# Gates A and B and the MLP's up projection as seven products of halves, with their splits spread over two units

## The chip, the cores and the metric

The kernel runs on one core of a Trainium2 chip. The metric is the device time of one execution in microseconds (us). The kernel before takes 857.63 us, the median of three runs (856.81 to 858.55).

## The reference

One encoder layer is applied to two groups of 256 tokens, so to 512 tokens of 1024 features, all in float32. Cut to what matters here:

```
proj = rms_norm(x) @ w_in          # q, k, v of three attention branches, and three gates ga, gb, gm of 1024 each
merged = sigmoid(ga) * (oa @ w_branch_a) + sigmoid(gb) * (ob @ w_branch_b) + sigmoid(gm) * (om @ w_branch_m)
x = x + merged @ w_out
x = x + square(relu(rms_norm(x) @ w_up)) @ w_down      # w_up 1024 x 4096, w_down 4096 x 1024
return rms_norm(x)
```

## The kernel before

**Layout and splits.** Activations stand with features on the 128 partitions and the 512 tokens along the free dimension. A float32 product is made of three matmuls in fp32r: every operand is split into a high part, which ScalarE (ACT) writes as a rounded copy, and a low part, which VectorE (DVE) writes as the operand less the high part. `mm3` issues high times high, high times low and low times high into one PSUM bank. `fm` runs `mm3` over the k tiles with a 128x128 piece of a weight as the stationary operand and all 512 tokens as the moving one. So a tile of 128 features costs 8 x 3 = 24 matmuls of 512 columns.

**Weights.** A weight comes in chunks of 128x1024 (512 KB) through SP's DMA queue into one of two `raw` buffers; ACT writes `hi`, then DVE `lo`, into ten `w` buffers (five chunks). During attention GpSimd (POOL) writes the `lo`s.

**Order of the work.** The program is one list of units, and `run` calls them in turn. Each unit may name sources; `run` fetches those of later units `ahead` sources early (three in the stages below). The engines are kept in the order of the calls (`InOrder`), so the order of the list is the order on PE, DVE and ACT. `later` holds evictions of a product until `flush` in the next unit; `lows` holds low parts until `lower()`, which `run` calls ahead of each unit.

**Gates and branches** (from 326 us on). Gate M was projected during attention. For each of eight feature tiles `ff` stand two units `gate` (24 matmuls of 512 columns each, then a sigmoid) and one unit `branches`, which multiplies the three attention outputs `OA`, `OB`, `OM` by their weights, times the gates. The sums go to POOL. `merge` splits the result into `M`; the last tile is split directly ahead of the output projection (`out_proj`), which reads all eight tiles.

**MLP.** The up projection makes 32 feature tiles (`up`, two halves of 12 matmuls each), four for each of eight blocks c of the down projection. The down projection of a block is seven products (Strassen's method on a 2 x 2 cut of tokens and features): `form` makes the activations' sums and differences, `parts` the weights' ones. There the weights' sums are made by DMAs that add onto a tile in SBUF (`accum_op`, on POOL's queue): `load_blocks` loads four blocks, and `T` grows block by block as its earlier products are split. Each product is 12 matmuls of 512 columns. A half of `up` and one `product` alternate; `add_to` adds the products into accumulators in SBUF. The last block c = 7 is multiplied directly (`last_down`), the sums enter the residual (`combine`, `sum_in`), and `finish`, `gained`, `factor` and `scale_out` make the final norm.

Of the kernel before, what the change touches and what calls it, by code (L numbers as in the profile page):

```python
# [16 lines left out]
P = 128  # L17
# [60 lines left out]
def encoder_kernel(ctx: ExitStack, tc: tile.TileContext, a: dict, out: bass.AP):  # L78
# [94 lines left out]
    def lower(keep=0):  # L173
        for fn in lows[:len(lows) - keep]:
            fn()
        del lows[:len(lows) - keep]

    def run():
        need = [(i, s) for i, (_, srcs) in enumerate(units) for s in srcs]
        got, at = [[] for _ in units], 0  # L180
        done = 0
        for i, (fn, srcs) in enumerate(units):
            done += len(srcs)
            for fetch in (True, False):
                while at < min(len(need), done + (0 if fetch else ahead[0])):
                    u, s = need[at]
                    got[u].append(s[0]() if callable(s[0]) else chunk(*s))
# [573 lines left out]

    MG, wb, sg = [], [], {}

    def gate(w, ff, br):
        p = bank()
        fm(w, X, p)
        g = h2("g")
        A.activation(g, p, AF.Sigmoid)
        sg[ff, br] = g

    def branches(w, *more):
        ff = len(MG)
        if more:
            wb[:] = more
        A.activation(GM[ff], GM[ff], AF.Sigmoid)
        sg[ff, 2] = GM[ff]
        c0 = (ff % 4) * 256
        parts = ((w[0][:, :512], w[1][:, :512], OA), (wb[0][0][:, c0:c0 + 256], wb[0][1][:, c0:c0 + 256], OB),
                 (w[0][:, 512:], w[1][:, 512:], OM))
        for br, (wh, wl, O) in enumerate(parts):  # L780
            p = bank()
            fm((wh, wl), O, p)
            V.tensor_tensor(sg[ff, br], p, sg[ff, br], op=ALU.mult)
        eng = V if ff == KD - 1 else G
        eng.tensor_tensor(sg[ff, 0], sg[ff, 0], sg[ff, 1], op=ALU.add)
        eng.tensor_tensor(sg[ff, 0], sg[ff, 0], sg[ff, 2], op=ALU.add)
        MG.append(sg[ff, 0])
# [3 lines left out]
    def merge(*ks):  # L791
        for k in ks:
            x = s4("mg")
            A.activation(x[:, 0], MG[k], AF.Copy)
            (V, G)[k % 2 if k < KD - 1 else 0].tensor_tensor(x[:, 1], MG[k], f(x[:, 0]), op=ALU.subtract)
            M.append(x)

    for ff in range(KD):
        for br in range(2):
            unit(lambda w, ff=ff, br=br: gate(w, ff, br), (a["w_g"][ff, br],))  # L800
        if ff == KD - 1:
            unit(lambda: merge(*range(KD - 1)))
        unit(branches, (a["w_bam"][ff],), *([(a["w_bb"][ff // 4],)] if ff % 4 == 0 else []))


    unit(lambda: merge(KD - 1))


    X1, H = [], []

    def out_proj(w):
        ff = len(H)
        r = h2("xr")
        A.dma_start(r, a["xT"][:, ff])
        p = bank()
        fm(w, M, p)
        V.tensor_tensor(r, p, r, op=ALU.add)
        X1.append(r)
        x = s4("h")
        A.activation(x[:, 0], r, AF.Copy, scale=gains[:, 2, ff:ff + 1])  # L820
        V.scalar_tensor_tensor(x[:, 1], r, gains[:, 2, ff:ff + 1], f(x[:, 0]), op0=ALU.mult,
                               op1=ALU.subtract)
        H.append(x)

    for ff in range(KD):
        unit(out_proj, (a["w_o"][ff],))

# [9 lines left out]

    def mlp_pool():
        stages.close()
        at[0] = stages.enter_context(tc.tile_pool(name="ml", bufs=1))

    def block_tile():
        return at[0].tile([P, 1024], F32, tag="blk", name=nm("blk"), bufs=8)
# [23 lines left out]
    def up(w, ff, half):  # L871

        if half == 0:
# [28 lines left out]
    def load_blocks(c):  # L902
# [3 lines left out]
        t = {n: block_tile() for n in "T2BC"}  # L906
        for n, b in (("T", "11"), ("2", "21"), ("C", "12"), ("B", "22")):
# [4 lines left out]
    def parts(c, n):  # L912

        def go():
            load_blocks(c)
            hi, lo = w_tile(), w_tile()
            src = blocks[c][n[0]]
            A.activation(hi, src, AF.Copy)

            def low():  # L920
                V.tensor_tensor(lo, src, f(hi), op=ALU.subtract)
                if n[1:]:
                    G.dma_start(src, block(c, n[1:]), accum_op=ALU.add)  # L923

            lows.append(low)
# [5 lines left out]
    def form(c, name):  # L931
# [11 lines left out]
        elif name == "Q5":  # L943
            src = forms[c, "S1"] = less(A21, A22)
        elif name == "Q6":
            src = forms[c, "S2"] = less(A11, forms.pop((c, "S1")))
        elif name == "P7":
            src = less(A11, A21)
        else:
            src = less(A12, forms.pop((c, "S2")))  # L950
        x = s4("f")
        xh, xl = (x[:, i].rearrange("p (j t) -> p j t", j=2) for i in range(2))
        A.activation(xh, src, AF.Copy)
        lows.append(lambda: V.tensor_tensor(xl, src, f(xh), op=ALU.subtract))
        forms[c, name] = x

    acc, banks = {}, {}
# [9 lines left out]
    PRODUCTS = dict(P1=("T12", "a", "V", -1), P2=("2", "a", "11", 1), Q5=("T22", "d", "G", 1),  # L967
                    Q6=("T21", "c", "V", 1), P7=("C", "e", "G", -1), Q3=("B", "d", "12", 1), Q4=("T", "e", "21", 1))

    def product(w, c, name):  # L970
        _, bk, to, sign = PRODUCTS[name]
# [47 lines left out]
    def last_down(hh, ts, n0=0, n1=512, part=0):  # L1019
        flush(9)  # L1020
        lower()
# [36 lines left out]
    unit(mlp_pool)  # L1058
    ORDER = ("P1", "P2", "Q5", "Q6", "P7", "Q3", "Q4")


    SUMMED = {1: ("12", "12"), 2: ("11", "11"), 3: ("21", "21"), 4: ("12", "V"), 5: ("21", "V", 1), 6: ("22", "G")}

    def make(c, n):
        unit(lambda: form(c, ORDER[n]))

    for c in range(NC):
        for h in range(8):
            ff, half = 4 * c + h // 2, h % 2
            unit(lambda *w, ff=ff, half=half: up(w[0] if w else None, ff, half), *([(a["w_up"][ff],)] if half == 0 else []))  # L1070
            if c == 0:
# [106 lines left out]
```

## Time and profile before

| | |
|---|---|
| median of three runs | 857.63 us |
| the profiled execution | 859.08 us |
| its span, first to last instruction | 857.3 us |
| mean granted TensorE clock | 0.993 |
| bytes moved by DMA | 106.87 MB |

The page of the profile lists for each engine the busy time, its share of the span and the instructions. PE is TensorE's matmuls, PEld its weight loads, which overlap the matmuls. A group row reads: line, engine, operation, output<-inputs, shapes, count | busy us, mean ns of one | idle time of the engine just before them, and what ended it. A row of the timeline reads: start, length, engine, operation, count, and in brackets the idle time before it with its releaser. Nearly all instructions have line 72, the helper that keeps the order; tiles tell them apart. A matmul's recorded length holds its way through the array, so the pace is read from start to start.

### The profile page before, as it was taken

How to read it: one execution, taken by the hardware profiler on the slowest of the kernel's cores; microseconds unless marked ns; L12 is line 12 of the kernel's file. 1: busy time of each engine (PE TensorE's matmuls, PEld its weight loads, DVE VectorE, ACT ScalarE, POOL GpSimd, SP SyncE). 2: the span in 40 equal slices, each digit the busy share in tenths (PEclk: the TensorE clock that was granted, in tenths of full speed). 3: DMA queues.
4: the chain of work that ended last, by engine and by line, in shares of the span. 5: the costliest groups of instructions: out<-in, count | busy, mean ns of one | idle time of the engine just before them, and what ended most of it. 6: DMA issues, size and time to landing. Idle time of an engine off the chain costs nothing.

```text
span 857.3 us, 10785 instructions
## 1 busy us (share of the span) xinstructions
PE 844.4 (99%) x4080; PEld 703.8 (82%) x4080; DVE 462.8 (54%) x737; ACT 397.1 (46%) x690; POOL 216.0 (25%) x161
## 2 busy tenths in 40 slices
PE   9999999999999999999999999999999999999996
PEld 7788998888888888888888788888888888888885
DVE  6575535465452311423435542465767666767895
ACT  6455545565554333222323227564445353545453
POOL 2314554656556543211123000000000000000001
PEclk9999999999999999999999999999999999999998
DMA  8343122324241228432322445374747465645322
GB/s 284 115 119 109 62 99 86 98 63 115 85 119 64 75 74 286 132 99 86 110 99 74 147 147 161 110 204 107 205 109 208 111 185 121 178 120 172 75 75 98
DMA packets 47468, 106.87 MB, mean 125 GB/s; under 512 B 19358, under 2 KB 19604, under 8 KB 47416
## 3 DMA queue, kind: packets, MB, share of 16 engines
q1 hardware_dynamic: 39992, 85.69, 30.2%
q0 software_dynamic: 4256, 14.73, 9.7%
q10 hardware_dynamic: 3168, 5.77, 2.0%
q8 instruction: 32, 0.52, 0.3%
q14 instruction: 20, 0.16, 0.1%
HBM read 101.93 MB, written 4.24 MB: 124 GB/s over the span
## 4 chain that ended last, share of the span: by engine, by line
PE 84%; DVE 8%; ACT 5%; issue 2%; DMA 1%; POOL 0%; POOLq 0%; SPq 0%; DVEq 0%; ACTq 0%
PE ps L72 77%; PE sc L72 3%; PE o L72 2%; DVE w L72 2%; PE tp L72 2%; ACT w L72 2%; DVE f L72 1%; ACT sp L72 1%; DVE sp L72 1%; DMA mr<-in_memT 1%; ACT f L72 1%; DVE sq L72 0%; ACT r L72 0%; DVE mg L72 0%; DVE acc L72 0%
## 5 line engine op out<-in xcount | busy, mean ns | idle before, releaser
L72 PE MATMUL ps<-x,w 128*128 128x512 f32 x1080 | 252.5, 391 | 0.0
L72 PEld LDWEIGHTS ps<-x,w 128*128 128x128 f32 x1080 | 201.0, 188 | 41.3
L72 PE MATMUL ps<-h,w 128*128 128x512 f32 x768 | 184.5, 391 | 0.0
L72 PEld LDWEIGHTS ps<-h,w 128*128 128x128 f32 x768 | 143.7, 188 | 29.5
L72 PE MATMUL ps<-w,f 128*128 128x512 f32 (+1 forms) x696 | 164.1, 387 | 1.3 <-DVE acc L72 1.0
L72 DVE TENSOR_TENSOR w<-raw,w 128x1024 fp32r<-128x1024 f32 (+1 forms) x79 | 96.4, 1223 | 115.3 <-ACT w L72 115.2
L72 PEld LDWEIGHTS ps<-w,f 128*128 128x128 f32 x696 | 128.7, 188 | 29.9 <-issue 3.4
L72 ACT ACTIVATE w<-raw 128x1024 fp32r<-128x1024 f32 (+2 forms) x116 | 119.7, 1036 | 21.9 <-DMA raw<-in_w_mem 7.5
L161 POOL TENSOR_TENSOR w<-raw,w 128x1024 fp32r<-128x1024 f32 (+1 forms) x37 | 87.3, 2361 | 120.1 <-ACT w L72 94.9
L72 DVE TENSOR_TENSOR w<-blk,w 128x1024 fp32r<-128x1024 f32 x49 | 59.5, 1224 | 47.7 <-ACT w L72 47.6
L923 POOL DMA_DIRECT2D blk<-in_w_dn x21 | 18.1, 864 | 240.2 <-DVE w L72 240.2
L72 ACT ACTIVATE w<-blk 128x1024 fp32r<-128x1024 f32 x49 | 50.7, 1047 | 15.4 <-DMA blk<-in_w_dn 15.4
L72 DVE TENSOR_TENSOR acc<-acc,ps 128x512 f32<-128x512 f32 x82 | 52.9, 682 | 2.9 <-PE ps L72 2.9
L72 ACT ACTIVATE f<-f 128x512 fp32r<-128x512 f32 x28 | 17.7, 633 | 75.4 <-DVE f L72 75.4
L72 ACT ACTIVATE sp<-sp,st 128x256 f32<-128x256 f32 (+1 forms) x48 | 25.8, 538 | 57.7 <-DVE st L72 57.7
L72 ACT ACTIVATE g<-ps 128x512 f32<-128x512 f32 x16 | 9.6, 598 | 88.4 <-PE ps L72 88.4
L72 DVE TENSOR_TENSOR sum<-o,lo 64x256 f32<-64x256 f32 x24 | 10.0, 417 | 66.5 <-ACT lo L72 66.3
L72 PE MATMUL ps<-mg,w 128*128 128x512 f32 x192 | 44.2, 391 | 1.5 <-ACT mg L72 0.9
L72 PEld LDWEIGHTS ps<-mg,w 128*128 128x128 f32 x192 | 36.0, 188 | 9.6 <-ACT mg L72 1.3
L72 ACT ACTIVATE r<-ps 128x512 f32<-128x512 f32 x32 | 18.9, 591 | 50.7 <-PE ps L72 50.7
L72 PE MATMUL ps<-w,x 128*128 128x384 f32 (+1 forms) x192 | 39.9, 363 | 0.0
L469 POOL TENSOR_TENSOR sp<-sp,st 128x512 f32<-128x512 f32 (+1 forms) x32 | 36.7, 1147 | 6.5 <-DVE st L72 3.6
(146 smaller groups left out, 959.2 us busy)
## 6 DMA issues: line engine op xcount, KB each, us to landing
raw<-in_w_up SPq DMA_DIRECT2D x32, 512.0 KB, 4.7
blk<-in_w_dn SPq DMA_DIRECT2D x28, 512.0 KB, 6.7
blk<-in_w_dn POOLq DMA_DIRECT2D x28, 512.0 KB, 5.7
raw<-in_w_g SPq DMA_DIRECT2D x24, 512.0 KB, 3.3
raw<-in_w_b SPq DMA_DIRECT2D x12, 512.0 KB, 3.3
raw<-in_w_bam SPq DMA_DIRECT2D x8, 512.0 KB, 3.3
raw<-in_w_o SPq DMA_DIRECT2D x8, 512.0 KB, 3.2
raw<-in_w_mem SPq DMA_DIRECT2D x7, 512.0 KB, 3.3
```

Source lines behind the costliest of these rows:

```text
L72: return self.tc.keep_in_program_order(method(*args, **kw))
L161: sub[0].tensor_tensor(lo[:, c], raw[:, c], f(hi[:, c]), op=ALU.subtract)
L469: G.tensor_tensor(s[:, :, :w], s[:, :, :w], st[:, 6:8].unsqueeze(2).to_broadcast([P, 2, w]), op=ALU.mult)
L923: G.dma_start(src, block(c, n[1:]), accum_op=ALU.add)
```

## The change

Gates A and B, and 28 of the 32 tiles of the up projection, are made as seven products of halves as well. `seven` takes four feature tiles at a time and cuts 1024 input features, 512 output features and 512 tokens into halves. One product is 24 matmuls with 256 tokens as the moving operand, seven products take the place of 96 matmuls of 512 columns. `halves_of` makes the four sums of the activations once for the gates and once for the up projection; `take` adds the products up. The weights' sums are DMAs that add onto a tile, as in the down projection; their rows come as two pieces of 512 columns. Gates run in two groups `q` of four tiles, A and B in turn; the four tiles of block c = 0 of `up` stay as they were.

The branch of M comes first, as eight units of its own (`memory_branch`), then gates of group 0, branches A and B, gates of group 1, branches A and B. The sums of the branches go from POOL to DVE. The first two tiles of `out_proj` are made together, the last two k tiles of both at the end. In the down projection two of the weight blocks come through `raw` in place of tiles of their own.

`lower` is replaced by `tick`, called at the start of a unit: it runs the weights' low parts (`wlows`), then the activations' low parts (`lows`), then the steps put off to ACT (`soon`). So a sum that DVE makes in one unit is copied by ACT in the next and lowered by DVE in the one after.

```diff
+    def tick():
+
+        for todo in (wlows, lows, soon):
+            now = todo[:]
+            todo.clear()
+            for fn in now:
+                fn()
...
+        def go(n, w):
+            tick()
+            new = n in ("P1", "Q5", "Q6", "P7")
+            if new:
+                banks[BANK[n]] = bank()
+            b = banks[BANK[n]]
+            for j in range(2):
+                for k in range(4):
+                    c = slice(j * 512 + k * P, j * 512 + (k + 1) * P)
+                    xh, xl = form_of(X, forms, n, k)
+                    mm3(b[:, j * S:(j + 1) * S], w[0][:, c], w[1][:, c], xh, xl, new and j == k == 0, k == 3, j > 0 or not new)
+            flush(9)
+            later.append(lambda: take(n, b))
...
+            elif n == "Q6":
+                v = e["21"] = room("21")
+                V.tensor_tensor(v, b, e["p"], op=ALU.subtract)
+                for m in ("12", "22"):
+                    V.tensor_tensor(e[m], e[m], v, op=ALU.add)
+                soon.append(lambda: put("12", e["12"]))
+            elif n == "P7":
+                V.tensor_tensor(e["22"], e["22"], b, op=ALU.subtract)
+                soon.append(lambda: put("22", e["22"]))
+            else:
+                V.tensor_tensor(e["21"], b, e["21"], op=ALU.subtract)
+                soon.append(lambda: put("21", e["21"]))
...
-        t = {n: block_tile() for n in "T2BC"}
-        for n, b in (("T", "11"), ("2", "21"), ("C", "12"), ("B", "22")):
+        t = {n: block_tile() for n in "TC"}
+        for n, b in (("T", "11"), ("C", "12")):
...
     def last_down(hh, ts, n0=0, n1=512, part=0):
         flush(9)
-        lower()
+        tick()
...
+    def put_last(i, h, r):
...
+        for j in range(2):
+            x, u, t = LAST[2 * h + j], r[:, j * S:(j + 1) * S], slice(i * S, (i + 1) * S)
+            A.activation(x[:, 0, t], u, AF.Copy)
+            lows.append(lambda x=x, u=u, t=t: V.tensor_tensor(x[:, 1, t], u, f(x[:, 0, t]), op=ALU.subtract))
```

Three places show what stands in the engines' order. First PE, at the first four k tiles of one up product; `h` is the normed activation, `w` the high and low parts of a weight. Before, two k tiles of a tile of `up`:

```order
L72 MATMUL ps_6771<-h_4103,w_6702 128x512 x2
L72 MATMUL ps_6771<-h_4103,w_6703 128x512
L72 MATMUL ps_6771<-h_4140,w_6702 128x512 x2
L72 MATMUL ps_6771<-h_4140,w_6703 128x512
L72 MATMUL ps_6771<-h_4177,w_6702 128x512 x2
```

After, at the same place of a product:

```order
L72 MATMUL ps_7246<-h_4636,w_7184 128x256 x2
L72 MATMUL ps_7246<-h_4636,w_7185 128x256
L72 MATMUL ps_7246<-h_4642,w_7184 128x256 x2
L72 MATMUL ps_7246<-h_4642,w_7185 128x256
L72 MATMUL ps_7246<-h_4685,w_7184 128x256 x2
```

The moving operand went from 512 to 256 columns; every matmul still has a weight load of its own.

Next DVE, at the start of a block of the down projection; `u` is the squared activation, `f` a form and its low part, `acc` the accumulators, `w<-raw` and `w<-blk` low parts of weights. Before:

```order
L72 TENSOR_TENSOR f_6203<-u_5954,u_6115 128x512
L72 TENSOR_TENSOR f_6205<-f_6203,f_6205 128x512
L72 TENSOR_TENSOR w_6223<-blk_5928,w_6222 128x1024
L72 TENSOR_TENSOR acc_4664<-acc_4664,ps_6208 128x512
L72 TENSOR_TENSOR acc_4666<-acc_4666,ps_6215 128x512
```

After:

```order
L72 TENSOR_TENSOR f_7280<-u_6952,u_7135 128x512
L72 TENSOR_TENSOR w_7274<-raw_7275,w_7273 128x1024
L72 TENSOR_TENSOR f_7278<-u_7135,f_7278 128x512
L72 TENSOR_TENSOR w_7303<-blk_7049,w_7302 128x1024
L72 TENSOR_TENSOR f_7282<-f_7280,f_7282 128x512
L72 TENSOR_TENSOR acc_5248<-acc_5248,ps_7286 128x512
L72 TENSOR_TENSOR acc_5250<-acc_5250,ps_7293 128x512
```

The low part `f_6205` of a difference stood right behind the difference; between `f_7280` and its low part `f_7282` now stand three other steps.

Last DVE at the end, around the first unit of `last_down`, whose two banks the first two rows read into the residual (`blk`); `rr` is a factor, `gf` the last gain, and the 256-column rows in `f` are the low parts of the last up product for tokens 256 to 511 (before, the last such row was `f_6823`, all 512 tokens of the last tile of `up`). Before:

```order
L72 TENSOR_TENSOR f_6823<-u_6756,f_6823 128x512
L72 TENSOR_TENSOR w_6854<-raw_6852,w_6853 128x1024
L72 TENSOR_TENSOR w_6860<-raw_6858,w_6859 128x1024
L72 SCALAR_TENSOR_TENSOR blk_6488<-ps_6826,rr,blk_6488 128x512
L72 SCALAR_TENSOR_TENSOR blk_6490<-ps_6827,rr,blk_6490 128x512
```

After:

```order
L72 TENSOR_TENSOR w_8117<-raw_8115,w_8116 128x1024
L72 TENSOR_TENSOR w_8123<-raw_8121,w_8122 128x1024
L72 SCALAR_TENSOR_TENSOR blk_7652<-ps_8089,rr,blk_7652 128x512
L72 SCALAR_TENSOR_TENSOR blk_7654<-ps_8090,rr,blk_7654 128x512
L72 TENSOR_TENSOR blk_7652<-blk_7652,gf_7660 128x512
L72 SCALAR_TENSOR_TENSOR blk_7656<-acc_5248,rr,blk_7656 128x512
L72 SCALAR_TENSOR_TENSOR blk_7658<-acc_5250,rr,blk_7658 128x512
L72 TENSOR_TENSOR f_7780<-e_7958,f_7780 128x256
L72 TENSOR_TENSOR f_7781<-e_7958,f_7781 128x256
```

The low parts moved behind the rows that read the banks of the first unit of `last_down`.

More of the change, by code (lines that the diff above doesn't have):

```diff
@@ L759, in encoder_kernel, with late_pool, block_tile @@
         unit(flush)
[L762 to L772 removed]
+    def late_pool():
+        stages.close()
+        at[0] = stages.enter_context(tc.tile_pool(name="ml", bufs=1))
+    def block_tile():
+        return at[0].tile([P, 1024], F32, tag="blk", name=nm("blk"), bufs=8)
+    SEVEN = ("P1", "P2", "Q5", "Q3", "Q6", "P7", "Q4")
@@ new lines, in encoder_kernel, with start_late, gates, block @@
+    MG, wb, sg = [], [], {}
+    XF = {}
+    def start_late():
+        late_pool()
+        for n in ("Q5", "Q6", "Q3"):
+            XF[n] = [at[0].tile([P, 1024], F32R, tag="blk", name=nm("f"), bufs=8) for _ in range(2)]
+    def gates(q, br):
+        def block(n):
+            k, f0 = int(n[0]) - 1, 4 * q + 2 * (int(n[1]) - 1)
+            return a["w_g"][f0:f0 + 2, br, :, k * 512:(k + 1) * 512].rearrange("f p c -> p f c")
+        def tiles():
+            if br == 0:
+                return block_tile(), block_tile()
+            return [sb.tile([P, 1024], F32, tag="s4", name=nm("wb"), bufs=21) for _ in range(2)]
+        both = {}
+        def room(n):
+            if n == "p":
+                return h2("e")
+            if n[1] not in both:
+                x = both[n[1]] = sb.tile([P, 2, T], F32, tag="s4", name=nm("g"), bufs=21)
+                for j in range(2):
+                    sg[4 * q + 2 * (int(n[1]) - 1) + j, br] = x[:, :, j * S:(j + 1) * S]
+            return both[n[1]][:, int(n[0]) - 1]
+        def put(n, x):
+            A.activation(room(n), x, AF.Sigmoid)
+        return seven(X, XF, block, tiles, put, room)
@@ L794, in merge @@
             A.activation(x[:, 0], MG[k], AF.Copy)
-            (V, G)[k % 2 if k < KD - 1 else 0].tensor_tensor(x[:, 1], MG[k], f(x[:, 0]), op=ALU.subtract)
+            V.tensor_tensor(x[:, 1], MG[k], f(x[:, 0]), op=ALU.subtract)
             M.append(x)
-    for ff in range(KD):
[L799 to L803, printed above, removed]
@@ L826, in encoder_kernel @@
+    unit(out_proj, *[(a["w_o"][ff],) for ff in range(2)])
+    for ff in range(2, KD):
         unit(out_proj, (a["w_o"][ff],))
@@ new lines, in make, with down_unit @@
+    def make(c, n):
+        unit(lambda: form(c, SEVEN[n]))
+    def down_unit(c, n):
+        for m in ((1, 2) if n == 0 else (n + 2,)):
+            if m < 7:
+                make(c, m)
+        unit(lambda w: product(w, c, SEVEN[n]), (parts(c, PRODUCTS[SEVEN[n]][0]),))
+    pieces_up = halves_of(H, HF)
+    for h in range(8):
+        ff, half = h // 2, h % 2
+        unit(lambda *w, ff=ff, half=half: up(w[0] if w else None, ff, half), *([(a["w_up"][ff],)] if half == 0 else []))
+        unit(lambda h=h: turn_x1(h % 4, h // 4))
+        if h == 0:
+            unit(start_up)
+        if h < 6:
+            unit(pieces_up[h])
+        if h == 1:
+            unit(lambda: load_blocks(0))
+            u7[1] = up_seven(1)
+            unit(u7[1][0])
```

282 lines of the change are left out of this document (216 added, 66 removed).

## The prediction

> **What bounds the kernel now.** I read the page first, then the table by stretches, then the groups by shape, then the timeline at the stages' seams, and last the DMA of two MLP blocks. The page's first part:
>
> ```profile
> PE 844.4 (99%) x4080; PEld 703.8 (82%) x4080; DVE 462.8 (54%) x737; ACT 397.1 (46%) x690; POOL 216.0 (25%) x161
> PE 84%; DVE 8%; ACT 5%; issue 2%; DMA 1%; POOL 0%; POOLq 0%; SPq 0%; DVEq 0%; ACTq 0%
> ```
>
> PE is busy for 99% of the span and holds 84% of the chain that ended last. The stretches (PE, PEld, DVE, ACT, POOL busy, clock, DMA share, GB/s) say the same of each stage: gates and branches, one MLP block, and the end.
>
> ```profile
> 326.50:472.30 145.80, 145.80 (x645) 120.79 (x643) 53.22 (x55) 44.23 (x59) 30.53 (x19) 1.00 0.37 123
> 588.20:629.40 41.20, 41.03 (x181) 33.73 (x180) 28.43 (x37) 19.34 (x26) 3.45 (x4) 1.00 0.58 153
> 794.40:857.30 62.90, 55.14 (x254) 45.76 (x252) 48.61 (x74) 28.07 (x48) 4.33 (x6) 0.96 0.29 84
> ```
>
> PE is full in the first two, and nothing else is near full: in an MLP block DVE works 28.4 of 41.2 us, ACT 19.3, the DMA engines 58%. So fewer PE cycles should shorten the time, until DVE or DMA fills up. Busy time is no measure of a matmul's pace; the timeline is, from start to start:
>
> ```profile
> 320.83 16.52 PE L72 MATMUL ps<-x,w 128*128 128x512 f32 x72
> 337.19 1.07 PE L72 MATMUL ps<-oa,w 128*128 128x512 f32 x4
> 847.03 2.68 PE L72 MATMUL ps<-w,f 128*128 128x256 f32 x21
> L72 PE MATMUL ps<-w,f 128*128 128x256 f32 x24 | 3.0, 283 | 0.0
> ```
>
> 72 matmuls of 512 columns take 337.19 - 320.83 = 16.36 us, 227.2 ns each. The 21 of 256 columns take 2.68 us with the last one's 0.283 us in it, so (2.68 - 0.283) / 20 = 119.9 ns each. That is more than half of 227.2: every matmul pays some 12 ns beside its columns.
>
> **The matmuls.** The order of PE has 384 fewer matmuls of 512 columns for the gates (1080 to 696) and 672 fewer for the up projection (768 to 96), and 384 + 672 + 792 = 1848 new ones of 256. Removed: 1056 x 227.2 = 239.9 us. Added: 1848 x 119.9 = 221.6 us. The difference is -18.3 us, all on the engine that sets the end; seven products for eight would give 12.5% of 239.9, or 30 us, if halving the columns halved the time. The Trainium skill, "TensorE: Matmul & The Clock Gate", section Back-to-back issue gap, puts the gap of isolated matmuls at the columns over 2.4 GHz plus 2.5 ns, so 109.2 and 215.8 ns; by that the saving would be an estimated 26.1 us. The rows above disagree with both figures, and I go by the rows.
>
> **Waits that go.** Two waits of PE stand at seams that the change rewrites. The first is the last tile of `merge` ahead of the output projection, the second the first product of each block:
>
> ```profile
> 467.75 4.92 PE L72 MATMUL ps<-mg,w 128*128 128x512 f32 x21
> 473.56 0.49 PE L72 MATMUL ps<-mg,w 128*128 128x512 f32 x1 [0.89 <-ACT mg L72]
> 474.64 3.69 PE L72 MATMUL ps<-mg,w 128*128 128x512 f32 x15 [0.58 <-DVE mg L72]
> 585.67 2.88 PE L72 MATMUL ps<-h,w 128*128 128x512 f32 x12
> 588.73 3.00 PE L72 MATMUL ps<-w,f 128*128 128x512 f32 x12 [0.17 <-DVE acc L72]
> 591.57 2.88 PE L72 MATMUL ps<-h,w 128*128 128x512 f32 x12
> ```
>
> From 467.75 to 474.64 stand 22 matmuls, 5.0 us of work in 6.89: 1.9 us lost. Now 36 matmuls (8.2 us) of the first two tiles need only earlier parts of `M`, and the chain behind the last branch (two products and two adds on DVE, a copy on ACT, a low part) is some 4 us long: the wait goes, -1.9. From 585.67 to 591.57 stand 24 matmuls, 5.45 us of work in 5.90: 0.45 us per block, seven blocks, 3.1 us. A block's first form is now made two units ahead of its product; I take 2.6 of the 3.1 and leave 0.5 for the entry of the first block, where a form still follows the last transposes closely.
>
> **What DVE gets.** Each of the seven groups of the up projection has three more low parts of weights (seven chunks for four) and five sums. DVE's pace, also from start to start:
>
> ```profile
> 649.92 1.22 DVE L72 TENSOR_TENSOR w<-raw,w 128x1024 fp32r<-128x1024 f32 x1
> 651.06 0.69 DVE L72 TENSOR_TENSOR f<-u,f 128x512 fp32r<-128x512 f32 x1
> 651.66 1.22 DVE L72 TENSOR_TENSOR w<-blk,w 128x1024 fp32r<-128x1024 f32 x1
> ```
>
> A low part of a chunk holds DVE for 1.14 us, a step of 512 columns for 0.60. A block gets 3 x 1.14 + 5 x 0.60 = 6.4 us more: 34.8 of DVE's time against 168 x 119.9 ns + 84 x 227.2 ns = 39.2 us of PE's, 89%. That is full but not over. Walking the order with these paces, two units lie between a low part and its product (5.6 us), and an eviction has one unit until its bank is added to again (2.7 us or more) with 1.4 to 2.1 us of DVE work ahead of it. So a steady block waits for nothing on DVE: 0. In the gates the load is lower (a low part per 2.88 us and 5 sums per seven products, so about 1.6 of 2.88). Ahead of the first gate product DVE has the sums of `X`, the forms' low parts, eight products of the branch M, their weights' low parts and three chunks: 30 steps of 512 columns, 28 of 256 (0.33, by the two paces) and three chunks, 30.6 us, against the last projection of attention and eight units of PE, (24 + 96) x 227.2 ns = 27.3 us, with weights three chunks ahead; I put 0.5 us there, between 0 and 4.
>
> The last block is over the line: besides 34.8 us it has ten sums into the residual and low parts of 256 columns, some 44 us against 39. What it is late by is bounded by those evictions; in the walk the adds on banks `e` come 0.4 to 0.8 us late: +1.0.
>
> **A new wait at the end.** The low parts of the last up product now stand on DVE behind rows that read the banks of the first unit of `last_down`, and the second unit's third matmul needs them. The same rows of before price this:
>
> ```profile
> 827.63 22.07 PE L72 MATMUL ps<-w,f 128*128 128x512 f32 x108
> 833.24 1.40 DVE L72 SCALAR_TENSOR_TENSOR blk<-ps,rr,blk 128x512 f32<-128x512 f32 x2
> 834.77 0.69 DVE L72 TENSOR_TENSOR blk<-blk,gf 128x512 f32<-128x512 f32 x1
> 835.38 1.41 DVE L72 SCALAR_TENSOR_TENSOR blk<-acc,rr,blk 128x512 f32<-128x512 f32 x2
> 836.71 0.75 DVE L72 SCALAR_TENSOR_TENSOR blk<-ps,rr,blk 128x512 f32<-128x512 f32 x1
> L72 DVE COPY pT<-tp 128x256 f32<-128x256 f32 x8 | 3.3, 415 | 0.0
> ```
>
> The first unit (24 matmuls from 827.63) ends at 833.08, and its successor's third matmul would start at 833.54. DVE is through with the five rows at 836.71, and a low part of 256 columns takes about 0.42: 837.13. So PE waits 3.6 us where before it waited for nothing, and it is the engine that ends last. DVE comes there late from the last block, +0.4. Sum: +4.0 us.
>
> **What the DMA engines get.** A group of the up projection had four plain chunks of 512 KB; now it has four plain ones and four that add onto a tile, and the down projection keeps four of each. Two blocks of before (640 to 722 us; packets, MB, share of 16 engines, then KB and us to landing):
>
> ```profile
> q1 hardware_dynamic: 2304, 8.39, 30.0%
> q0 software_dynamic: 1134, 4.12, 29.2%
> blk<-in_w_dn POOLq DMA_DIRECT2D x8, 512.0 KB, 6.5
> DMA to landing us min/median/max: 2.0/5.7/9.5
> ```
>
> Eight adding transfers took 29.2% of 82 us, 2.99 us of all engines each; the 16 plain ones 30.0%, 1.54 us each. Four and eight made 4 x 2.99 + 8 x 1.54 = 24.3 us, the 58% of the stretch. Eight and eight make 8 x 2.99 + 8 x 1.54 = 36.2 us of 39.2, 92%. So they fit, narrowly. The chain that a late landing would hold is copy, low part, add onto the tile, next copy, over four chunks or 11.2 us; beside 6.5 us of landing it has ACT's copy, DVE's low part and POOL's issue (the fourth row is an eviction by ACT):
>
> ```profile
> L72 ACT ACTIVATE w<-blk 128x1024 fp32r<-128x1024 f32 x49 | 50.7, 1047 | 15.4 <-DMA blk<-in_w_dn 15.4
> L72 DVE TENSOR_TENSOR w<-blk,w 128x1024 fp32r<-128x1024 f32 x49 | 59.5, 1224 | 47.7 <-ACT w L72 47.6
> L923 POOL DMA_DIRECT2D blk<-in_w_dn x21 | 18.1, 864 | 240.2 <-DVE w L72 240.2
> L72 ACT ACTIVATE g<-ps 128x512 f32<-128x512 f32 x16 | 9.6, 598 | 88.4 <-PE ps L72 88.4
> ```
>
> That is 6.5 + 1.05 + 1.22 + 0.86 = 9.6 us; landings up to 8 us are hidden, and weights run three chunks ahead. I put 1.5 us, between 0 and 8. ACT gets three copies of chunks and three evictions more per block, 3 x 1.05 + 3 x 0.60 = 5 us on 19.3: it has room.
>
> **The sum**, against the profiled execution (859.08 us: span 857.3 and 1.8 around): -18.3 - 1.9 - 2.6 + 0.5 + 1.0 + 4.0 + 1.5 = -15.8, so 843.3 us. That execution lies 1.45 us above the median of the runs shown; beside the median the forecast is 842.
>
> **Rivals.** First, DMA becomes the bound, which ends slower. The adding transfers of `w_up` and `w_g` come in pieces of 2 KB, where all adding ones of before had 4 KB. If an adding packet costs by the piece and not by the byte, four transfers of a group cost 5.98 us each, and a block's DMA 4 x 5.98 + 4 x 2.99 + 8 x 1.54 = 48.2 us: nine over 39.2, seven times, about 905 us. It decides from (39.2 - 12.0 - 12.3) / 4 = 3.7 us per such transfer, and the gain is gone from about 4.3. Against it: plain pieces of 2 KB cost by the byte. In the first 21 us, filled mostly with 2 KB rows, the engines moved 284 GB/s at 8 tenths, some 350 at full share, and the two blocks above give 8.39 MB in 24.6 us, 341.
>
> ```profile
> DMA  8343122324241228432322445374747465645322
> GB/s 284 115 119 109 62 99 86 98 63 115 85 119 64 75 74 286 132 99 86 110 99 74 147 147 161 110 204 107 205 109 208 111 185 121 178 120 172 75 75 98
> ```
>
> Second, DVE sets the pace of the MLP: 89% leaves 4.4 us per block for its waits, and in before it sat idle 12.8 us per block, part of it for ACT (47.6 us ahead of the 49 low parts above). If 1.5 us per block come out of PE, seven blocks cost 10: 852 us, still faster.
>
> Third, short matmuls do not hold 119.9 ns over long runs. For it: this group in the attention is slower, and one pair of others faster.
>
> ```profile
> L72 PE MATMUL sc<-mk,qm 128*128 128x256 f32 x48 | 7.5, 293 | 0.0
> 319.55 0.40 PE L72 MATMUL o<-pT,vb 128*128 128x256 f32 x2
> ```
>
> 7.5 / 48 = 156 ns, with the ends of its groups in it; at that price 1848 x 36 ns = 67 us would be lost, 909 us. The pair gives 0.40 - 0.28 = 0.12 us, no less than mine. The Trainium skill, the same page, section Part 3: Packing small matmuls, The mechanism, says that a weight load overlaps with matmuls in flight only where the row groups differ, which would end slower here; the 24 short matmuls above, each with a full load, run at 119.9 ns and speak against it. Fourth, all new waits are hidden but the one at the end: 842 - 0.5 - 1.0 - 1.5 = 839.
>
> **Chances and range.** The forecast (840 to 848, by the bounds of gate entry, last block and DMA) 0.68; all hidden (836 to 840) 0.11; DVE's pace (848 to 856) 0.10; DMA 0.05 and slow short matmuls 0.02, both slower; 0.04 that several of these together bring the old time back, 0.03 of it within 0.2%. 0.2% of 857.63 is 1.7 us, about what a measurement can tell. Faster: 0.89; same 0.03; slower 0.08. The range reaches from 836 to 850.
>
> **What would show it.** After, long runs of short matmuls at 120 ns, 24 in 2.88 us; blocks of about 39.5 us; no wait at `mg`; one PE wait of 3 to 4 us for `f` some 20 us ahead of the end; DVE near 35 us per block. Blocks above 41 us with ACT waiting on `blk` would be the first rival, with DVE lacking idle time the second. A time above 850 makes the prediction wrong.

## The result and the profile after

The changed kernel takes 878.93 us (median of four runs, 878.58 to 880.1) where the kernel before takes 858.09 us in the same set: 1.025 times as long, 95% interval 1.0236 to 1.0264. The forecast was 842. The profiled execution after is 878.92 us long, with a span of 877.1, against 859.08 and 857.3 before. The first part of its page and its chain by engine:

```profile
PE 840.6 (96%) x4872; PEld 733.1 (84%) x4872; DVE 583.6 (67%) x941; ACT 460.3 (52%) x788; POOL 235.0 (27%) x185
PE 45%; issue 17%; DVE 15%; DMA 15%; ACT 6%; POOL 1%; SPq 0%; POOLq 0%; DVEq 0%; ACTq 0%
```

PE is busy for 96% in place of 99%, and it holds 45% of the chain that ended last in place of 84%. DMA, which held 1%, holds 15%. The stretches (PE, PEld, DVE, ACT, POOL busy, clock, DMA share, GB/s) show where: the gates, one block of the MLP, the end.

```profile
326.50:478.00 151.50, 143.70 (x926) 131.43 (x925) 105.98 (x149) 71.93 (x102) 22.30 (x19) 0.95 0.72 181
650.00:691.00 41.00, 39.55 (x253) 35.67 (x252) 34.45 (x45) 23.96 (x32) 8.40 (x8) 1.00 0.90 206
816.00:877.00 61.00, 46.69 (x244) 39.57 (x242) 45.25 (x72) 23.83 (x45) 4.63 (x6) 0.91 0.27 78
```

DVE is busy 34.45 us in the block (34.8 were forecast) and the DMA engines 90% (92%). The loads came out as worked out; PE's waits did not. The short matmuls hold their pace: 24 of them without a wait are a row of 3.04 us, (3.04 - 0.283) / 23 = 119.9 ns each, as forecast.

```profile
673.14 3.04 PE L72 MATMUL ps<-h,w 128*128 128x256 f32 x24
```

So the 18.3 us are saved, and lost again in waits. This is PE's timeline at the five kinds of place (start, length, and in brackets the idle time with what ended it):

```profile
337.70 7.67 PE L72 MATMUL ps<-om,w 128*128 128x512 f32 x20 [3.36 <-ACT w L72]
...
463.91 0.80 PE L72 MATMUL ps<-oa,w 128*128 128x512 f32 x1 [4.44 <-DVE w L72]
...
565.56 4.63 PE L72 MATMUL ps<-f,w 128*128 128x256 f32 x24 [3.77 <-ACT e L72]
...
694.32 1.89 PE L72 MATMUL ps<-w,f 128*128 128x512 f32 x7 [1.29 <-DVE acc L72]
...
850.88 1.65 PE L72 MATMUL ps<-w,f 128*128 128x512 f32 x3 [4.07 <-DVE f L72]
```

The first row holds more than a wait: 20 matmuls take 7.67 us, (7.67 - 0.39) / 19 = 383 ns each in place of 227. The 24 short ones from 565.56 take 4.63 us in place of 3.04. After the long waits PE runs at half speed for a while: the granted clock is 0.50 from 337.7 to 343.5 us, and 0.95 over the stretch from 326.5 to 478, where it was 1.00 before.

Taking each matmul's start to the next one's start and summing what lies over 227.2 or 119.9 ns gives, from 320 us on, 43.1 us after and 5.8 us before. 43.1 - 5.8 - 18.3 = +19.0 us, against 878.92 - 859.08 = +19.8 measured. By place (us; 2.7 of the 43.1 lie in gaps too small to list):

| place | wait | half speed behind it | in the prediction |
|---|---|---|---|
| products of branch M, 334 | 3.5 | 3.0 | gate entry, +0.5 (0 to 4) |
| branches behind the second gates, 459 | 4.6 | 3.0 | nothing |
| first two products of `out_proj`, 478 and 492 | 0.9 | | none left |
| first up block of seven, 561 | 3.9 | 1.6 | nothing |
| blocks, 600 to 820 | 12.0 | | DMA +1.5 (0 to 8), DVE 0, last block +1.0 |
| last up product, 833 | 1.3 | | in the last block's 1.0 |
| last down projection, 846 | 4.2 | 2.4 | +4.0 |

### The profile page after: what moved, and what is told of

The parts are those of the page before. It is cut to its first block, busy times and chain, and to the rows that moved or that the text cites. A ratio compares the mean times of both kernels' runs of the same rounds, so it can differ in the third digit from the quotient of the medians.

```text
span 877.1 us, 12822 instructions
## 1 busy us (share of the span) xinstructions
PE 840.6 (96%) x4872; PEld 733.1 (84%) x4872; DVE 583.6 (67%) x941; ACT 460.3 (52%) x788; POOL 235.0 (27%) x185
## 4 chain that ended last, share of the span: by engine, by line
PE 45%; issue 17%; DVE 15%; DMA 15%; ACT 6%; POOL 1%; SPq 0%; POOLq 0%; DVEq 0%; ACTq 0%
PE ps L72 39%; DMA blk<-in_w_dn 6%; DMA blk<-in_w_up 6%; DVE w L72 4%; PE sc L72 3%; ACT w L72 3%; PE o L72 2%; DVE acc L72 2%; DVE f L72 2%; PE tp L72 2%; DVE blk L72 2%; DMA mr<-in_memT 1%; DVE e L72 1%; DMA raw<-in_w_mem 1%; ACT sp L72 1%
## 5 line engine op out<-in xcount | busy, mean ns | idle before, releaser
L72 PE MATMUL ps<-x,w 128*128 128x512 f32 (+1 forms) x1080 | 211.0, 353 | 0.0
L72 PEld LDWEIGHTS ps<-x,w 128*128 128x128 f32 x1080 | 175.2, 189 | 26.7
L72 ACT ACTIVATE w<-raw 128x1024 fp32r<-128x1024 f32 (+2 forms) x116 | 112.2, 977 | 50.3 <-DMA raw<-in_w_bam 21.1
L72 DVE TENSOR_TENSOR w<-blk,w 128x1024 fp32r<-128x1024 f32 x80 | 97.8, 1222 | 42.1 <-ACT w L72 42.0
L72 PE MATMUL ps<-h,w 128*128 128x256 f32 (+1 forms) x768 | 109.5, 298 | 1.1 <-DVE e L72 1.1
L72 ACT ACTIVATE w<-blk 128x1024 fp32r<-128x1024 f32 x80 | 82.7, 1051 | 52.4 <-DMA blk<-in_w_dn 40.0
L72 PEld LDWEIGHTS ps<-h,w 128*128 128x128 f32 x768 | 101.2, 191 | 8.3 <-issue 3.1
L72 PEld LDWEIGHTS ps<-f,w 128*128 128x128 f32 x792 | 98.5, 193 | 7.8 <-ACT e L72 6.5
L72 PE MATMUL ps<-f,w 128*128 128x256 f32 x792 | 99.9, 285 | 4.8 <-ACT e L72 4.7
L873 POOL DMA_DIRECT2D blk<-in_w_up x21 | 25.3, 1204 | 191.3 <-DVE w L72 181.7
L72 PE MATMUL ps<-w,x 128*128 128x384 f32 (+1 forms) x192 | 39.9, 363 | 0.0
L1142 POOL DMA_DIRECT2D blk<-in_w_dn x21 | 21.5, 1024 | 60.6 <-DMA blk<-in_w_up 41.0
```

The costliest lines, as they stand in the source:

```text
L72: return self.tc.keep_in_program_order(method(*args, **kw))
L873: G.dma_start(by2(src), block(ONTO[n]), accum_op=ALU.add)
```

## The experiments

Blocks are counted from the start of the first up product of a block to that of the next; those of c = 2 to 6 are "steady". After, five of them take 208.3 us, 41.66 each. No kernel below differs from the changed one but by its edit, and each was timed beside the kernel before on the same chip (857.2 to 858.3 us there).

### The steady blocks: take away the new adding transfers, or some of DVE's work

```diff
-            G.dma_start(by2(t["C"]), block("22"), accum_op=ALU.add)
+            if adds:
+                G.dma_start(by2(t["C"]), block("22"), accum_op=ALU.add)
...
-                if n in ONTO:
+                if adds and n in ONTO:
...
-        return seven(H, HF, block, lambda: (block_tile(), block_tile()), put)
+        return seven(H, HF, block, lambda: (block_tile(), block_tile()), put, adds=False)
```

> Leaves out the adding transfers of w_up in the up blocks of seven products (three onto T and one onto C per block), so those products use unsummed weights; every instruction of PE, DVE and ACT stays, and the down projection and the gates keep their adds. In the changed kernel the steady MLP blocks take 41.66 us each (five from 609.25 to 817.53) where the matmuls alone are 39.2. Theory A (late landings: eight adding transfers per block fill the DMA engines to 88%, ACT's copy waits for a landing, and all that stands behind it on ACT and DVE is late): the blocks fall to 39.2 to 39.9 us, ACT's wait ahead of its copies from blk falls from 52 us to under 15, total 863 to 868. Theory B (DVE's own load, 34 of 41 us, and the order of its queue hold PE): blocks stay above 41.2 us, total 875 to 879.

Measured: 864.67 us, 1.0076 (1.0049 to 1.0102). Steady blocks take 39.34 us each. The stretch of five of them:

```profile
589.00:785.70 196.70, 196.70 (x1262) 179.50 (x1261) 171.49 (x219) 120.67 (x162) 16.32 (x19) 1.00 0.63 161
```

And its group of ACT's copies from `blk` (busy us, mean ns, idle us ahead of them):

```profile
L72 ACT ACTIVATE w<-blk 128x1024 fp32r<-128x1024 f32 x80 | 81.9, 1051 | 5.1 <-DMA blk<-in_w_g 4.8
```

PE is busy in all 196.70 us, with the same 171.5 us of DVE work as before the edit (171.25, below), and ACT's wait ahead of its copies from `blk` falls from 52.4 us to 5.1. Theory A, the late landings, holds, and 39.34 is what such a block costs with all waits hidden.

```diff
-            hi, lo = w_tile(), w_tile()
+            hi = w_tile()
+            lo = hi if X is H and n in ("P2", "Q3") else w_tile()
...
+                if X is H:
+                    A.activation(hi, src, AF.Copy)
+                    return hi, hi
```

(and the same in `parts` for the blocks "21" and "22")

> Leaves out the low parts of the weights of P2 and Q3 in the MLP (the high part is used twice), so DVE has four chunk steps of 1.14 us less per block, some 29.8 us in place of 34.3, and all transfers stay. Theory A (late landings of the adding transfers): blocks stay at 41.3 to 41.7 us, total 876 to 879. Theory B (DVE's load and queue): blocks fall to 39.2 to 39.9 us, total 862 to 868.

Measured: 863.17 us, 1.0058 (1.0039 to 1.0077). Steady blocks take 40.33 us: neither 41.3 to 41.7 nor 39.2 to 39.9. The first up block gained 4.1 us, and the stretch from the start of the last block to the end of the kernel 3.5, of which 0.7 us are less half speed behind the wait at its end, where the edit does not act. Neither theory alone has this. The stretch of five steady blocks after, ACT's copies there in the whole run, and DVE's waits in the stretch (us in total, times, longest):

```profile
589.60:797.90 208.30, 200.18 (x1261) 179.10 (x1260) 171.25 (x219) 120.84 (x162) 41.76 (x40) 1.00 0.88 203
```

```profile
L72 ACT ACTIVATE w<-blk 128x1024 fp32r<-128x1024 f32 x80 | 82.7, 1051 | 52.4 <-DMA blk<-in_w_dn 40.0 <-DMA blk<-in_w_up 8.3 <-DMA blk<-in_w_g 4.1
```

```profile
DVE w L72 <- ACT w L72: 36.7, 21, 3.5
```

The same stretch and copies without the raw low parts:

```profile
584.00:785.70 201.70, 199.82 (x1262) 179.12 (x1261) 149.36 (x199) 120.86 (x162) 41.79 (x40) 1.00 0.90 209
```

```profile
L72 ACT ACTIVATE w<-blk 128x1024 fp32r<-128x1024 f32 x80 | 82.9, 1052 | 51.2 <-DMA blk<-in_w_dn 41.9 <-DMA blk<-in_w_up 6.2 <-DMA blk<-in_w_g 2.9
```

After, DVE works 171.25 / 5 = 34.25 us per block and waits 36.7 / 5 = 7.3 us for ACT's copies: 41.6, the length of the block. To fit into 39.34 it may wait 5.1 us. Without the raw low parts ACT waits for the same landings (51.2 us), but DVE has 29.9 us of work and stands the wait. So the landings are late, and DVE's load is why PE feels it: the theory from here on is the two together, AB.

### Why the landings are late

The timeline of POOL, SP, ACT and DVE at one block shows it (rows of other tiles are left out). L858 loads C of the next up block, L859 is the transfer that adds onto it, L1142 the one that adds onto T of the down projection:

```profile
666.73 0.38 SPq L858 DMA_DIRECT2D blk<-in_w_up  x1
...
668.73 1.20 POOL L873 DMA_DIRECT2D blk<-in_w_up  x1 [2.07 <-DVE w L72]
669.61 1.23 DVE L72 TENSOR_TENSOR w<-blk,w 128x1024 fp32r<-128x1024 f32 x1
...
673.19 1.20 POOL L859 DMA_DIRECT2D blk<-in_w_up  x1 [3.26 <-DMA blk<-in_w_up]
673.91 1.42 POOL L1142 DMA_DIRECT2D blk<-in_w_dn  x1
...
684.07 1.06 ACT L72 ACTIVATE w<-blk 128x1024 fp32r<-128x1024 f32 x1 [6.30 <-DMA blk<-in_w_dn]
685.16 1.23 DVE L72 TENSOR_TENSOR w<-blk,w 128x1024 fp32r<-128x1024 f32 x1 [3.01 <-ACT w L72]
```

The low part that L1142 needs is done at 669.61 + 1.23 = 670.84. But POOL stands at L859, which needs C's load, issued only at 666.73: it waits 3.26 us. L1142 goes out at 673.91, 3.1 us late and as the third adding transfer within 5.2 us, and ACT can copy at 684.07, 10.2 us later. C itself is wanted a whole block later. The next kernel makes L859 wait, through a copy of one column on DVE, until the adding transfers of the block are out:

```diff
+            if X is H and started[0]:
+                pend.append(held_add)
+            else:
+                add()
+
+        def add():
             G.dma_start(by2(t["C"]), block("22"), accum_op=ALU.add)
+
+        def held_add():
+            V.tensor_copy(t["C"][:, :1], t["C"][:, :1])
+            add()
...
+                if n == "T21":
+                    while pend:
+                        pend.pop(0)()
```

> Same work and one one-column copy more on DVE per block, which stands behind the low part of Q6's weights of the down projection; the transfer that adds onto C for the next up block waits for it. In the changed kernel three adding transfers stand one behind the other once per block (668.73, 673.19 and 673.91 in one block, 709.78, 715.23 and 715.95 in the next), and the last, onto T of the down projection, lands 9.8 and 10.0 us after its issue; ACT's copy waits for it and DVE behind that. Theory A1 (the place in the adding queue is what makes the landings late): that transfer lands in 7 us or less, blocks fall from 41.66 to 39.4 to 40.5 us, total 867 to 873. Rival (the engines are 88% full, so another transfer is late in its place): blocks stay at 41.3 to 41.9, total 877 to 880.

Measured: 864.52 us, 1.0087 (1.0072 to 1.0102), 14.4 us less than the change, more than expected. Steady blocks: 39.34 us, 5 x 2.32 = 11.6 of the 14.4; the wait at 459 and the half speed behind it lost 3 us as well, since the edit also takes an adding transfer away from there (see the gates, below). The same place in the timeline:

```profile
659.25 0.90 POOL L1134 DMA_DIRECT2D blk<-in_w_dn  x1 [9.46 <-DMA blk<-in_w_up]
660.54 1.20 POOL L883 DMA_DIRECT2D blk<-in_w_up  x1 [0.39 <-DVE w L72]
661.42 1.23 DVE L72 TENSOR_TENSOR w<-blk,w 128x1024 fp32r<-128x1024 f32 x1
662.95 0.90 POOL L1152 DMA_DIRECT2D blk<-in_w_dn  x1 [1.21 <-DVE w L72]
...
666.05 2.19 PE L72 MATMUL ps<-h,w 128*128 128x256 f32 x17
```

The stretch of five blocks, and ACT's and DVE's waits in it:

```profile
587.40:784.10 196.70, 196.70 (x1262) 179.55 (x1261) 171.81 (x224) 121.86 (x162) 41.33 (x39) 1.00 0.93 216
```

```profile
ACT w L72 <- DMA blk<-in_w_dn: 8.0, 5, 1.9
DVE w L72 <- ACT w L72: 20.3, 16, 1.7
```

The transfer goes out 0.3 us behind its low part and 3.1 us ahead of the block's first product (666.05), where it went out 0.8 us behind that (673.14). ACT waits 8.0 us in five blocks for `w_dn` in place of 40.0, DVE 20.3 / 5 = 4.1 us per block in place of 7.3. The bytes are the same and the engines now 93% busy: DMA bandwidth is not what holds these blocks. The landing itself was not always 7 us or less as expected, since two others (659.25 and 660.54) still go ahead of it. From issue to landing, L1142 of the change and then the same line, L1152, of this kernel:

```profile
DMA to landing us min/median/max: 5.3/7.1/12.5
```

```profile
DMA to landing us min/median/max: 5.2/5.7/9.4
```

How much is due to POOL standing still and how much to the places among the adding transfers was not separated.

```diff
-            V.tensor_tensor(d, u, v, op=ALU.subtract)
+            G.tensor_tensor(d, u, v, op=ALU.subtract)
```

> Same work; the four subtractions per block that make the forms of the down projection go from DVE to POOL, 4 x 0.60 = 2.4 us less of DVE's 34.3 us per block. Theory AB (late landings take from DVE about 7 us per block of waiting, and with 34.3 us of load that no longer fits into 39.2): the blocks shorten as they did without the raw low parts, 1.33 us for 4.6 us, so by 0.7 us each, to 40.9 to 41.1 us, total 873 to 876. Rival (POOL takes 1.3 to 2.1 us for such a step and issues the adding transfers behind it, later than now): blocks of 41.6 us or more, total 878 to 882.

Measured: 879.52 us, 1.0274 (1.0247 to 1.03). The total is the rival's, but the steady blocks, 41.28 us, lie between the two ranges, and the first up block lost 2.8 us more. A step of 0.60 us on DVE takes 1.6 to 2.1 us on POOL (medians of the three kinds among the 28). That this makes the adding transfers late is not shown; in the rows at hand POOL waits for DVE ahead of them. What the trace shows is that DVE's own steps take longer while POOL computes (L1157 is the moved subtraction; the last row is the five steady blocks):

```profile
676.65 3.43 DVE L72 TENSOR_TENSOR w<-raw,w 128x1024 fp32r<-128x1024 f32 x1
676.87 2.13 POOL L1157 TENSOR_TENSOR f<-u,u 128x512 f32<-128x512 f32 x1
679.08 3.86 POOL L1157 TENSOR_TENSOR f<-u,f 128x512 f32<-128x512 f32 x2
680.01 1.78 DVE L72 TENSOR_TENSOR f<-u,f 128x512 fp32r<-128x512 f32 x1
592.70:799.10 206.40, 198.94 (x1261) 180.03 (x1260) 182.19 (x199) 121.05 (x162) 73.33 (x60) 1.00 0.88 205
```

The low part of 1.22 us takes 3.43 there, the step of 0.69 us 1.78. With 20 steps fewer, DVE is busy for 182.19 us in five blocks, where it was busy for 171.25.

### The gates and the first up block

This is what stands ahead of the waits at 334 and 459 in the change (rows of other tiles are left out; L992 loads `w_bam`, L859 at 451.38 adds onto C of the up block c = 2, whose first product starts at 589.63):

```profile
335.20 1.28 ACT L72 ACT_TABLE_LOAD   x1
337.03 0.61 ACT L72 ACTIVATE w<-raw 128x512 fp32r<-128x512 f32 x1
...
451.38 1.20 POOL L859 DMA_DIRECT2D blk<-in_w_up  x1 [1.75 <-DMA blk<-in_w_up]
453.34 0.33 SPq L992 DMA_DIRECT2D raw<-in_w_bam  x1
459.57 0.63 ACT L72 ACTIVATE w<-raw 128x512 fp32r<-128x512 f32 x1 [4.86 <-DMA raw<-in_w_bam]
460.75 2.50 DVE L72 TENSOR_TENSOR mg<-q,mg 128x512 fp32r<-128x512 f32 x4 [5.51 <-ACT mg L72]
463.17 1.28 DVE L72 TENSOR_TENSOR w<-raw,w 128x512 fp32r<-128x512 f32 x2
```

At 334 the copy of the weights stands on ACT behind copies of forms that wait for DVE, and behind a table load of 1.28 us and a sigmoid. At 459 two things meet: the weights are copied only 6.2 us after the issue of their load, and then their low part stands on DVE behind four parts of `merge`. The late load goes with the adding transfer at 451.38. Up to this place six kernels differ in the adding transfers of `w_up` alone. Where the one at 451.38 goes out there (the change, `no_raw_lows`, `tail_tick`, `forms_pool`), the weights are copied 6.2 to 6.5 us after the issue and PE waits 4.6 to 4.8 us. Where it does not (`c_add_held`, `no_up_adds`), they are copied after 4.5 and 3.2 us, and PE waits 3.0 and 1.3 us; some of this comes back at `mg` (2.0 and 3.3 us there, 0.4 to 2.0 in the other four).

```diff
-    for br in range(2):
-        unit(g4[0, br][0])
-    for i in range(4):
-        unit(pieces[i])
-        unit(tick)
...
-        if ff < 4:
-            unit(pieces[4 + ff])
+        if ff in (1, 2):
+            unit(g4[0, ff - 1][0])
+        unit(pieces[ff])
...
+            if q and n in (3, 4, 5, 6):
+                unit(lambda: merge(len(M)))
...
-            if ff == 4:
-                unit(lambda: merge(*range(4)))
```

> Same work; ahead of the gates the pieces of the forms of X go one behind each product of the branch M instead of four ahead of them all, the first loads of T and C come two and three of those products later, and the first four parts of merge go one behind each of the gate units n = 3 to 6 of the second group instead of all behind the fifth branch. In the changed kernel PE waits at 333.95 (3.5 us and 3.0 us of half-speed matmuls behind it) and at 459.08 (4.6 and 3.0). Theory C (order: the copies of weights stand on ACT behind copies of forms that DVE has not made, and the low part of weights on DVE behind the four parts of merge): both waits fall below 1.5 us and the half speed with them, total 864 to 868. Rival (DVE has too much to do in these stretches wherever it stands, or the loads of w_bam land late): one or both waits stay above 3 us, total 871 to 879.

Measured: 874.8 us, 1.0192 (1.0167 to 1.0216). Both waits are gone, 14.1 us with their half speed, and 11.2 us came back at 350 to 356 and at 467 to 472:

```profile
350.85 2.89 PE L72 MATMUL ps<-x,w 128*128 128x256 f32 x22 [0.94 <-DVE w L72]
356.05 2.34 PE L72 MATMUL ps<-x,w 128*128 128x256 f32 x12 [2.31 <-ACT e L72]
...
472.49 1.80 PE L72 MATMUL ps<-mg,w 128*128 128x512 f32 x4 [3.23 <-DVE mg L72]
```

So a place in the order held PE, but DVE was behind with its work, and what stood next in its queue was late instead. To see whether DVE's work is the cause, some of it is left out, with the order as in the change:

```diff
-        wlows.append(lambda: V.tensor_tensor(lo[:, :512], raw[:, :512], f(hi[:, :512]), op=ALU.subtract))
-        return hi[:, :512], lo[:, :512]
+        return hi[:, :512], hi[:, :512]
...
+        if late[0]:
+            A.activation(hi[:, :n], raw[:, :n], AF.Copy)
+            return hi, hi
```

> Leaves out the low parts of the weights that come through raw from the last projections of the attention up to the first half of the up projection (w_bam, w_bb, w_o, the first four chunks of w_up; the high part is used twice); order and transfers stay as in the changed kernel. PE waits there at 333.95 (6.5 us with the half speed behind it), 459.08 (7.6) and 561.41 (5.5). Theory C1 (DVE has more to do in these stretches than fits): all three fall below 1.5 us, total 858 to 863. Rival (the order of ACT's queue and the landings hold them): at least two stay above 3 us, total 870 to 877.

Measured: 863.82 us, 1.0072 (1.005 to 1.0093). The wait at 334 falls from 6.5 us with its half speed to 0.8, that at 459 goes; the one at the first up block stays as it was:

```profile
334.54 1.67 PE L72 MATMUL ps<-om,w 128*128 128x512 f32 x6 [0.68 <-ACT w L72]
...
551.42 1.86 PE L72 MATMUL ps<-f,w 128*128 128x256 f32 x7 [3.76 <-ACT e L72]
```

C1 holds for the gates and falls for the first up block. (Without its low part a chunk also leaves its `raw` buffer sooner, so that loads go out earlier; this run does not separate that from DVE's time.) There ACT's eviction of the third product (Q5), which the fourth (Q3) adds to, stands behind copies of forms that DVE makes at that moment: a matter of order.

> Same work; the run gates_spread with, besides, half of the sums for the forms of X and H and the adds of the gated branches (but the last) on POOL in place of DVE, and the last two pieces of the forms of H one up product later. In gates_spread PE still waited at 349.6 and 353.5 (5.2 us with the half speed) and at 467.3 and 468.8 (6.0), and at 556.8 ahead of the second product of the first up block (5.5). Theory C1 (DVE has too much to do in these three stretches): each falls below 2 us, total 861 to 866. Rival (the order or the landings of w_bam and w_o hold them, not DVE's load): at least two of them stay above 3 us, total 870 to 876.

(The product named last there is the fourth, not the second.) Edit: `gates_spread`, with `(V, G)[i]` for `V` in the sums of `halves_of`, `G` for `V` in the second line of `gated` for ff < 7, and the last two pieces of the forms of H behind the up products n = 2 and 3. Measured: 878.33 us, 1.0252 (1.023 to 1.0274), no gain at all. The waits at 349 to 354 (5.4 us), at `mg` (6.6 with the half speed) and in the first up block (3.1 and 1.6 behind it, now at 580) stay above 3 us. Giving DVE's work to POOL did not help at any place where it was tried. Here too DVE is slower beside POOL's steps: ahead of the wait at `mg` the low parts at 461.97 and 465.24 take 2.00 and 2.34 us in place of 1.22.

### The end

```diff
     def last_down(hh, ts, n0=0, n1=512, part=0):
+        tick()
         flush(9)
         tick()
```

> Same work; in the last down projection the deferred low parts are issued ahead of the rows that finish a unit, not behind them. In the changed kernel PE waits 4.2 us at 846.4 and then runs ten matmuls at half speed, 2.4 us. Theory D (that low part stands on DVE behind five rows that it does not need): the wait falls below 1.6 us and the half speed goes, total 873 to 875. Rival (DVE is late with everything in the last block, so the wait stays where the low part is): wait of 3 us or more, total 877 to 879.

Measured: 872.34 us, 1.0169 (1.0146 to 1.0193), 6.6 us less than the change, against 4 to 6 expected. The last 120 matmuls, 96 of 512 columns and 24 of 256, run through: 96 x 227.2 + 24 x 119.9 ns = 24.7 us of work in a row of 24.91.

```profile
837.51 24.91 PE L72 MATMUL ps<-w,f 128*128 128x512 f32 x120
```

Theory D holds, and the 2.4 us of half speed go with the wait.

### Versions to beat both

> Same work; gates_pool, tail_tick, c_add_held and forms_pool together. If the waits are separate, their gains add: 878.9 less 6.6 (tail, measured), 13 to 18 (gates and first block), 4 to 10 (steady blocks): 845 to 855, faster than the kernel before at 858. Rival (relieving one place moves the wait to the next on the same engine, DVE or POOL): 858 to 866.

Edit: `gates_pool`, `tail_tick`, `c_add_held` and `forms_pool`. Measured: 855.14 us, 0.9974 (0.9958 to 0.999), just past the upper end of what was expected if gains add; two of its parts had gained nothing.

> Same work; c_add_held, tail_tick and gates_spread together, nothing moved to POOL. If the gains add: 878.9 - 14.4 - 6.6 - 4.1 = 853.8, so 852 to 856. Rival (they overlap): 857 to 861, no faster than the kernel before.

Measured: 851.02 us, 0.993 (0.9913 to 0.9947). The gains add, with 3 us more. In `gates_spread` alone the five steady blocks take 210.8 us and not 208.3, so there were 14.1 us to gain in them in place of 11.6. The wait at `mg`, 6.0 us with its half speed there, is 1.8 here; of the two edits that came on top only the held transfer can act at that place (in `gates_spread` it goes out at 449.01, ahead of the last load of `w_bam`).

```diff
-        unit(pieces[ff])
+        if ff < 6:
+            unit(pieces[ff])
...
+            if q == 0 and n in (2, 3):
+                unit(pieces[4 + n])
...
-            if c == 1 and n in (1, 2):
-                unit(pieces_up[5 + n])
+            if c == 1 and n in (2, 3):
+                unit(pieces_up[4 + n])
```

> mended_b0 with the last two pieces of the forms later: of X behind the gate units n = 2 and 3 of the first group instead of the last two products of the branch M, of H behind n = 2 and 3 of the first up block instead of 1 and 2. Theory C2 (the pieces, made early, stand on DVE and ACT ahead of steps that PE needs sooner): the waits near 349 to 354 (5.2 us) and 557 to 561 (5.5) fall below 2 each, total 845 to 849. Rival (the same steps are late wherever the pieces stand, or the seventh form becomes late): 852 to 857.

Measured: 844.66 us (842.6 to 846.32), 0.9847 (0.9828 to 0.9867): faster than both kernels, and near the forecast for the change itself. PE's waits from the gates on:

```profile
PE ps L72 <- DVE e L72: 2.8, 2, 1.6
PE ps L72 <- DVE acc L72: 2.2, 2, 1.6
PE ps L72 <- DVE mg L72: 1.2, 1, 1.2
PE ps L72 <- ACT e L72: 0.8, 1, 0.8
PE ps L72 <- DVE g L72: 0.7, 1, 0.7
```

By the same count from start to start 10.9 us are left of 43.1, no wait is over 1.8 us, and no long half speed follows. C2 holds: with nothing taken from DVE, the order alone hides its work, the order of the adding transfers included. That also settles the gates: DVE's backlog there has room, if pieces that are wanted later stand later.

> mended_b1 with the low parts of w_bb, w_o and the first four chunks of w_up on POOL in place of DVE (2.36 us there for 1.14 on DVE). Theory C1 (DVE's load in the branches, the output projection and the first up units): the wait at mg (some 6 us in gates_spread) falls below 2, total 4 us or more below mended_b1. Rival (POOL is late with them, or its adding transfers stand behind them): no faster than mended_b1 by more than 1 us, or slower.

Edit: the switch of `chunk`'s low parts back to DVE stands behind the first half of the up projection in place of ahead of the gates. Measured: 850.64 us, 0.991 (0.9893 to 0.9928), 6 us more than `mended_b1`: two waits at `mg` (3.4 and 1.8 us, 1.6 of half speed) and 1.7 us in small ones ahead of the first down products come back. The rival holds, by two ways: ahead of the first wait a step of DVE takes 2.12 us in place of 0.69 (at 465.64, beside a low part on POOL from 464.87 to 467.22), and the second wait ends with a low part on POOL.

## Why the prediction was wrong, step by step

**The matmuls, -18.3: right.** 119.9 ns hold wherever PE does not wait, so the third rival falls.

**The merge wait, -1.9, and the block's first product, -2.6: nearly right.** 0.9 us stayed at `out_proj`, and no wait is left at a block's first down product. But the step counted the seams that the change removes and not those that it makes.

**Gate entry, +0.5 between 0 and 4: mis-sized, and two seams left out.** It cost 6.5. The sum set 30.6 us of DVE work against 27.3 of PE's, so a wait of some 3 us at the end of it could at most be left. PE waited in the middle, for a copy of weights that stood on ACT behind copies of forms and a table load. The same kind of wait came at the branches (7.6, with a late load of `w_bam` and then four parts of `merge` ahead of its low part on DVE) and at the first up block (5.5). Neither of these two had a term. Without DVE's low parts the first two go (`no_late_lows`), in another order no single wait of the three places is over 1.8 us (`mended_b1`).

**"Landings up to 8 us are hidden" and "a steady block waits for nothing on DVE": these failed.** The landing was taken as 6.5 us from before, with four adding transfers per block. With eight, POOL's order counts: the transfer that adds onto C holds POOL for its own load, and that onto T goes out 3.1 us late and lands 10.2 us later. This costs 2.3 us per block (41.66 against 39.34), 11.6 in five. The Trainium skill, "DMA: Bandwidth & Descriptors", section Issuing engines are not separate DMA queues, holds the time that the issuing engine needs to be usually small beside the DMA; here the 1.2 us are, but not the 3.26 us for which POOL stood waiting to issue.

**The rivals.** The first, DMA as the bound, is right about the place (ACT waiting on `blk`) and wrong about the cause: adding pieces of 2 KB cost by the byte (the row below, of the change from 640 to 722 us, has 58.8% of the engines for 8.25 MB, half of it in such pieces, where before it was 29.2% for 4.12 MB), and with the engines 93% busy the blocks still take 39.34 us. The second is the nearest: DVE's 4.4 us to spare against 7.3 us of waits for ACT. Its price was 1.5 us per block, and 2.3 were measured. No case had both with the seams, which took the sum from -15.8 to +19.8.

```profile
q0 software_dynamic: 3292, 8.25, 58.8%
```

**The end, +4.0: right in kind.** The wait is 4.2 us for `f`, with 3.6 + 0.4 worked out, and ends 26 us ahead of the end (some 20 were named). What was missing is the half speed behind it, 2.4 us. The last block's +1.0 became 3.1 (1.8 of the 12.0 in the table, and 1.3), and it stays, at 2.5 to 3.1 us, in every kernel here but `no_raw_lows` (0.5).

**The half speed had no term.** Four waits, 16.2 us in all, brought 10.0 us of it.

## What to carry to other kernels

When an in-order engine gets near its full load, count its waits as well as its work: 34 us of work in 39 leave 5 us, and one late transfer takes more. A transfer that is wanted late must not stand ahead of one that is wanted soon on the queue that issues them, above all if it has to wait for a load of its own. For each new seam write down what stands ahead of the awaited step on each queue it passes, before any sum of loads is believed; here moving steps of the order gained 34 us, and moving work to another engine none, since POOL took longer for it and slowed DVE's own steps meanwhile.

## What the runs showed of the hardware

After a wait of PE, matmuls ran at about 427 in place of 227 ns (213 in place of 120 for the short ones). In the change and the twelve runs, from 320 us on and counted from start to start, no wait up to 2.03 us was followed by that; of 39 waits from 2.35 us on, 37 were, mostly with 8 to 17 slow matmuls and 1.3 to 3.0 us lost. In the change the granted clock is then 0.50 for 6.83 us (from 337.02, 463.31 and 849.02) or 3.41 us (from 565.71). The Trainium skill, "TensorE: Matmul & The Clock Gate", section Why this matters for your kernels, asks for no idle gap over some 3 us; the traces agree in kind, but here 2.35 us was already too long.

POOL needs 1.6 to 2.1 us (medians in `forms_pool`) for a float32 step of 128x512 that DVE does in 0.60. While POOL computes, DVE's steps on two tiles in SBUF slow down: in `forms_pool` from 326.5 us on, the 16 low parts of 128x1024 that lie mostly beside a step of POOL take 2.3 us in the median, the others 1.22; the adds of a PSUM bank onto `acc` stay at 0.68 us beside POOL.
